# A four-layer trunk on one core: where residual, raw weights and split weights of the up products lie in SBUF, and five weight buffers in place of six

## The chip, the core and the metric

The kernel runs on one core of a Trainium2 chip. A core has TensorE (PE: matmuls from SBUF into PSUM; PEld is its loading of the stationary operand), VectorE (DVE), ScalarE (ACT), GpSimd (POOL) and SyncE (SP). SP, POOL and ACT also issue DMA transfers. Each engine works through its own instructions in order and waits for the others through semaphores. The metric is the device time of one execution in microseconds.

## What is computed

```python
# x: (1, 512, 1024) float32; two layers, mixer 0 = MLA, mixer 1 = GLA
for i in range(2):
    xn = rms_norm(x, norm_mix[i])
    x = x + (mla_mixer(xn, ...) if i % 2 == 0 else gla_mixer(xn, ...))
    x = x + sq_relu_mlp(rms_norm(x, norm_mlp[i]), mlp_w_up[i], mlp_w_down[i])
return rms_norm(x, final_norm)

def sq_relu_mlp(xn, w_up, w_down):          # w_up (1024, 4096), w_down (4096, 1024)
    return jnp.square(jax.nn.relu(xn @ w_up)) @ w_down
```

All is float32. The change lies in the two MLPs and in where some tiles lie.

## The kernel before, in words

**Numbers as two parts.** TensorE is fed tiles of a rounded type (F32R). A float32 tile is split in two: ACT copies it into the rounded type (`hi`, L104), DVE subtracts that from the source (`lo`, L107). A product of two such pairs is three matmuls: hi by hi, hi by lo, lo by hi (L112 to L114, and the same in L939, L948 and elsewhere). Weights come by DMA as float32 into `wraw` (`load`, L132, two buffers of 8 KB a partition) or, in the MLPs, into `comb` buffers; `piece` (L137) splits them into a pair of tiles `wh`, `wl`, of which there are three pairs of 4 KB tiles, taken in turns. A split for one product therefore waits until the product three before it is done.

**The pools.** Tiles are laid out from the low end of SBUF: `const` (among it the residual `xall`, 16 KB a partition, L155), then `sb` (wraw, wh, wl, `set_A` for activations' two parts, `set_B`, `tmp`, `acc` and small ones), and behind it whatever stage is running: the pools of MLA, `fast0` of the first MLP, the pool of GLA, `fast1` of the second MLP.

**An MLP.** 512 hidden columns make a block, of which there are eight. The first block's up product is done plainly (`up_first`, L846). Then come seven steps (`step`, L951). A step makes the up product of block b+1 and the down product of block b, each of them a 2 by 2 product of quadrants worked out with seven products in place of eight (a Strassen-Winograd scheme); sums of quadrants are formed on DVE, or by a transfer that adds to what is there (POOL, `accum_op=ALU.add`, L918 and L928). A step has 14 products, in turns up and down:

1 up a11, 2 down d11, 3 up a12, 4 down d12, 5 up a11 (now S1 + a11) with T2, 6 down d11 (now dS1 + d11), 7 up S1 with T1, 8 down d12 (now d11 + d12), 9 up a12 (now a11 + a12), 10 down dS3, 11 up s3 with T3, 12 down dS1, 13 up a22 with T4, 14 down d22.

An up product (`up_product`, L931) is 24 matmuls, L939, with 256 columns of a moving activation and a stationary weight tile. The moving tile is a `set` tile in 1, 3 and 9 and a `T` tile in 5, 7, 11 and 13. A down product (`down_product`, L941) is 12 matmuls, L948, with 512 columns of a moving weight tile and a stationary activation.

T1 to T4 are sums of the normed input's quadrants. `quadrants` (L864) forms them once in each MLP: float32 values t1 to t4 first (L873 to L877), in the buffers comb 2 to 5, then `signed` splits each (L828, L829) into the tiles T2, T3, T1, T4.

**The weights of a step.** Six comb buffers hold six of the pieces (S1, dS1, d11, d12, dS3, d22); A1 and A2 (1 MB each) go through wraw. `home` says which piece is in which buffer (L911). S1, dS1, dS3 and A2 have a second transfer that is added to the first, on POOL's queue. When a piece's last reader in a step has been issued, `after(name)` (L1098) fetches a piece of the next step into its buffer, by the table `NEXT` (L1056); the plain transfers go through SP's queue in the order of these calls. Before the first step the pieces are fetched in the order of the list in L1051; the first MLP also writes the residual to DRAM there (L1054), since the residual's own tile then serves for the sums S11, S12, SU, S21 (L814). A fifth sum, S5, has a tile of its own (L815).

**Ends of an MLP.** In the last step `before_next` (first MLP, L1070) or `at_the_end` (second, L1080) fetches other things into buffers that come free: the residual kept in DRAM, or the last block's down weights and the final gain. The last block is then done plainly: L1126 to L1136 in the first MLP, where L1135 adds the kept residual; `row` (L1162) in the second.

**GLA.** `pairs` (L1392) copies with a mask; the mask is an integer copy of the identity, `ident_i` (L1669). L1515 and, in `states`, L112 to L114 are matmuls with 256 columns there, on tiles S, qd, ADh, ADl, kth, ktl of its pool.

The order of the instructions on each engine, and the buffers that tiles get, come from a planner that walks the program with a model of the times; where it finds a product's operands late it puts another one first.

Of the kernel before, what the change touches and what calls it, by code (L numbers as in the profile page):

```python
# [50 lines left out]
def trunk_kernel(ctx: ExitStack, tc: tile.TileContext, t_in: dict, out: bass.AP):  # L51
# [4 lines left out]
    sb = ctx.enter_context(tc.tile_pool(name="sb", bufs=1))  # L56
    count = [0]
# [97 lines left out]
    xall = const.tile([P, ND, S], F32, name="xT")  # L155
# [218 lines left out]
    def mla(layer, nrm, first, pools):  # L374
# [37 lines left out]
        raw = sb.tile([P, ND, 256], F32, tag="wraw", bufs=2, name=uname("wraw"))  # L412
# [54 lines left out]
        raw = sb.tile([P, 2, MH, VD], F32, tag="wraw", bufs=2, name="wraw_v")  # L467
# [61 lines left out]
        raw = sb.tile([P, 3, MH, ROPE], F32, tag="wraw", bufs=2, name="wraw_qr")  # L529
# [18 lines left out]
        def project(h, tag="a"):  # L548
            if h % 4 == 0:
                raw = sb.tile([P, 3, 4, NOPE], F32, tag="wraw", bufs=2, name=uname("wraw_qn"))  # L550
# [3 lines left out]
                raw = sb.tile([P, 2, 4, NOPE], F32, tag="wraw", bufs=2, name=uname("wraw_kn"))  # L554
# [244 lines left out]
    def mlp(layer, nrm, nxt=None):  # L799
# [64 lines left out]
        def quadrants():  # L864
# [4 lines left out]
            t1, t2, t3, t4 = (by_k(comb(i), KH) for i in range(2, 6))  # L869
# [8 lines left out]
            for name, t, sign in (("T2", t2, -1.0), ("T3", t3, 1.0), ("T1", t1, -1.0), ("T4", t4, -1.0)):  # L878
                parts = fast.tile([P, KH, 2, TH], F32R, tag=name, name=uname(name))
                signed(t, parts[:, :, 0], parts[:, :, 1], sign)  # L880
                quad[name] = [parts[:, k] for k in lead]
# [29 lines left out]
        home = {"S1": 0, "dS1": 1, "d11": 4, "d12": 3, "dS3": 2, "d22": 5}  # L911
# [19 lines left out]
        def up_product(t, a, q, start):  # L931
            w = piece(a, KH, 256)
# [7 lines left out]

        def down_product(t, a, parts, start):  # L941
            wh, wl = piece(a, 2, 512)
# [8 lines left out]
        def step(b, q, r, after):  # L951
# [23 lines left out]
            d11, d12, ds1, ds3, d22 = (W[n] for n in ("d11", "d12", "dS1", "dS3", "d22"))  # L975
# [68 lines left out]
            onto("d", S21, d22, parts_of_quad(q21, -1.0), opening)  # L1044
# [25 lines left out]
        def before_next(name):  # L1070
            if name in ("d11", "S1", "d12", "dS3"):
                t = by_k(comb(home[name]), 2)
                SP.dma_start(t, x_kept[:, 2 * len(kept) : 2 * len(kept) + 2])
                kept.append(t)
            if name in ("A1", "A2"):
                last_raw.append(load(down_cols(len(last_raw)), 4, 512))
            if name == "dS1":
                DVE.tensor_tensor(S12, S12, S5, ALU.add)

        def at_the_end(name):  # L1080
            if name in ("d11", "S1", "d12", "dS3"):
                i = len(last_raw)
                t = by_k(comb(home[name]), 2)
                k0 = (NB - 1) * FB + i % 2 * 256
                SP.dma_start(t, w_dn[k0 : k0 + 256, i // 2 * 512 : (i // 2 + 1) * 512].rearrange("(k p) n -> p k n", p=P))
                last_raw.append(t)
            if name == "dS1":
                DVE.tensor_tensor(S12, S12, S5, ALU.add)
                t = comb(home[name])
                SP.dma_start(t, t_in["fin_row"].to_broadcast([P, D]))  # L1090
                gain.append(t)
                rounded(0)
# [16 lines left out]
        if nxt:  # L1109
# [5 lines left out]
            DVE.scalar_tensor_tensor(SU, SU, -1.0, S5, ALU.mult, ALU.subtract)  # L1115
# [27 lines left out]
        DVE.tensor_tensor(SU, SU, S5, ALU.add)  # L1143
# [53 lines left out]
    def gla(layer, nrm, vtag, ytag):  # L1197
# [165 lines left out]
        def levels(h):  # L1363
# [28 lines left out]
            def pairs():  # L1392
# [4 lines left out]
                def evacuate(p, a):  # L1397
                    DVE.copy_predicated(a, ident_i.unsqueeze(1).to_broadcast([P, 2, P]), p[:, :, :P])
# [232 lines left out]
    raw0 = sb.tile([P, ND, 256], F32, tag="wraw", bufs=2, name="wraw_ckv")  # L1631
# [37 lines left out]
    ident_i = const.tile([P, P], I32, name="ident_i")  # L1669
    DVE.tensor_copy(ident_i, ident)  # L1670
# [73 lines left out]
```

## Time and profile before

| | |
|---|---|
| median of 3 runs | 1057.02 us (1056.98 to 1057.12) |
| the profiled execution | 1057.37 us, of which its span 1055.6 us |
| TensorE clock granted | 0.999 |
| MLA and its output projection, up to the first MLP's steps | 0 to 206 us |
| steps of the first MLP | 206 to 480 us, 39 us each |
| GLA and its output projection | 505 to 752 us |
| steps of the second MLP | 753 to 1027 us |
| last block and final norm | 1027 to 1055.6 us |

How rows are read: a row of instructions has line, engine, operation, out<-in by the tiles' names, shapes and count, then busy time in us, mean ns of one, and idle time of the engine just before with what ended it. A row of a timeline begins with start and duration in us and ends with the idle time before it in brackets. "PE ps L939 x24" in the chain of waits is a run of 24 matmuls with the time from the first start to the next piece. A row of a window has its length, then PE, PEld, DVE, ACT and POOL busy time, then clock, share of DMA engines and GB/s.

### The profile page before, as it was taken

The page shows a single profiled execution, that of the slowest core. Times are in us where ns is not written, and L with a number is a line of the kernel's source. Part 1 is how long each engine was busy: PE and PEld are TensorE (multiplying, and loading weights), DVE is VectorE, ACT ScalarE, POOL GpSimd, SP SyncE. Part 2 cuts the span into 40 slices and gives each one's busy share as a digit, 9 for nine tenths or more (in the row PEclk, how much of TensorE's full clock was granted, in tenths as well). Part 3 has the DMA queues.
Part 4 walks back from the last instruction along what each step waited for, and adds up shares of the span by engine and source line. Part 5 has one row for each costly group of instructions (what it writes and reads, how often), then busy time and mean ns, then how long its engine had stood idle before and what let it go on. Part 6 is the DMA issues. An engine that isn't in the chain of part 4 may idle for free.

```text
span 1055.6 us, 15598 instructions
## 1 busy us (share of the span) xinstructions
PE 1045.5 (99%) x5966; PEld 913.7 (87%) x5966; DVE 876.0 (83%) x1340; ACT 698.6 (66%) x1074; POOL 113.4 (11%) x128
## 2 busy tenths in 40 slices
PE   9999999999999999999999999999999999999997
PEld 7888888889999999998888888878889999999985
DVE  7899977979889889898686498469889989989993
ACT  7667664577777767766445565655667777777784
POOL 7410011201101111000000000000011010010000
PEclk9999999999999999999999999999999999999999
DMA  7311235866966976842322221444496696696622
GB/s 231 90 51 41 81 79 160 238 176 150 235 181 150 229 192 146 221 147 93 90 80 80 80 80 51 126 105 132 110 248 132 178 254 140 176 249 152 165 81 80
DMA packets 120493, 149.97 MB, mean 142 GB/s; under 512 B 9345, under 2 KB 86145, under 8 KB 120289
## 3 DMA queue, kind: packets, MB, share of 16 engines
q1 hardware_dynamic: 95920, 117.76, 34.4%
q0 software_dynamic: 22400, 29.36, 17.4%
q10 hardware_dynamic: 2096, 1.84, 0.6%
q8 instruction: 47, 0.77, 0.3%
q14 instruction: 30, 0.24, 0.1%
HBM read 144.49 MB, written 4.19 MB: 141 GB/s over the span
## 4 chain that ended last, share of the span: by engine, by line
PE 95%; ACT 2%; DVE 2%; issue 0%; DMA 0%; ACTq 0%; SPq 0%; DVEq 0%
PE ps L939 26%; PE ps L948 25%; PE ps L112 10%; PE ps L114 10%; PE ps L113 10%; PE ps L1133 2%; PE ps L1388 2%; PE ps L129 1%; PE ps L1168 1%; PE ps L408 1%; PE ps L1515 1%; DVE wl L107 0%; PE ps L671 0%; PE ps L1438 0%; PE ps L667 0%
## 5 line engine op out<-in xcount | busy, mean ns | idle before, releaser
L948 PE MATMUL ps<-wh,set 128*128 128x512 f32 x784 | 258.5, 390 | 0.0
L107 DVE TENSOR_TENSOR wl<-wraw,wh 128x1024 fp32r<-128x1024 f32 x139 | 169.4, 1221 | 39.7 <-ACT wh L104 39.4
L104 ACT ACTIVATE wh<-wraw 128x1024 fp32r<-128x1024 f32 x139 | 145.9, 1053 | 82.1 <-PE ps L113 38.3
L948 PEld LDWEIGHTS ps<-wh,set 128*128 128x128 f32 x784 | 147.3, 188 | 28.8
L104 ACT ACTIVATE wh<-comb 128x1024 fp32r<-128x1024 f32 x112 | 118.8, 1061 | 62.8 <-PE ps L939 41.9
L939 PE MATMUL ps<-T,wh 128*128 128x256 f32 x896 | 159.8, 279 | 0.0
L948 PE MATMUL ps<-wl,set 128*128 128x512 f32 x392 | 153.7, 392 | 0.0
L107 DVE TENSOR_TENSOR wl<-comb,wh 128x1024 fp32r<-128x1024 f32 x112 | 136.7, 1220 | 18.6 <-ACT wh L104 16.9
L939 PEld LDWEIGHTS ps<-T,wh 128*128 128x128 f32 x896 | 140.5, 188 | 4.5
L939 PE MATMUL ps<-T,wl 128*128 128x256 f32 x448 | 125.1, 279 | 1.0 <-DVE wl L107 1.0
L939 PE MATMUL ps<-set,wh 128*128 128x256 f32 x672 | 122.6, 283 | 0.0
L939 PEld LDWEIGHTS ps<-set,wh 128*128 128x128 f32 x672 | 107.4, 191 | 3.2
L112 PE MATMUL ps<-set,wh 128*128 128x512 f32 x280 | 109.3, 392 | 0.7 <-ACT set L1557 0.3
L113 PE MATMUL ps<-set,wh 128*128 128x512 f32 x280 | 109.4, 391 | 0.0
L114 PE MATMUL ps<-set,wl 128*128 128x512 f32 x280 | 109.0, 390 | 0.0
L939 PE MATMUL ps<-set,wl 128*128 128x256 f32 x336 | 95.2, 283 | 0.0
L939 PEld LDWEIGHTS ps<-T,wl 128*128 128x128 f32 x448 | 84.2, 188 | 1.5 <-DVE wl L107 1.4
L948 PEld LDWEIGHTS ps<-wl,set 128*128 128x128 f32 x392 | 73.8, 188 | 11.6
L928 POOL DMA_DIRECT2D comb<-in_mlp_w_down_dram x28 | 33.6, 1201 | 421.0 <-DMA comb<-in_mlp_w_down_dram 155.5
L939 PEld LDWEIGHTS ps<-set,wl 128*128 128x128 f32 x336 | 64.3, 191 | 0.0
L112 PEld LDWEIGHTS ps<-set,wh 128*128 128x128 f32 x280 | 52.5, 188 | 12.6 <-ACT wh L104 1.0
L114 PEld LDWEIGHTS ps<-set,wl 128*128 128x128 f32 x280 | 52.6, 188 | 11.2 <-DVE wl L107 0.4
(396 smaller groups left out, 2024.2 us busy)
## 6 DMA issues: line engine op xcount, KB each, us to landing
comb<-in_mlp_w_down_dram SPq DMA_DIRECT2D x74, 512.0 KB, 5.0
wraw<-in_mlp_w_up_dram SPq DMA_DIRECT2D x32, 1024.0 KB, 5.8
comb<-in_mlp_w_down_dram POOLq DMA_DIRECT2D x28, 512.0 KB, 7.7
wraw<-in_gla_w_in_dram SPq DMA_DIRECT2D x12, 1024.0 KB, 5.3
comb<-in_mlp_w_up_dram SPq DMA_DIRECT2D x14, 512.0 KB, 3.8
comb<-in_mlp_w_up_dram POOLq DMA_DIRECT2D x14, 512.0 KB, 8.4
wraw<-in_mlp_w_up_dram POOLq DMA_DIRECT2D x14, 512.0 KB, 7.2
wraw<-in_mla_w_o_dram SPq DMA_DIRECT2D x4, 1024.0 KB, 5.0
```

The source lines that it names most:

```text
L104: order(ACT.activation(hi, src, AF.Copy))
L107: lo_eng.tensor_tensor(lo, src, f(hi), ALU.subtract)
L112: PE.matmul(psum, wh, xh, start=start, stop=False)
L113: PE.matmul(psum, wh, xl, start=False, stop=False)
L114: PE.matmul(psum, wl, xh, start=False, stop=stop)
L129: PE.transpose(psum, src, ident[: src.shape[0], : src.shape[0]])
L408: PE.matmul(p, w[:, i, j * P : (j + 1) * P], x, start=start, stop=stop)
L928: POOL.dma_start(t, q(b, *more), accum_op=ALU.add)
L939: PE.matmul(o, a_, x_, start=start and j == 0 and k == 0 and n == 0, stop=k == KH - 1 and n == 2, skip_group_check=True)
L948: PE.matmul(o, x_, w_, start=start and k == 0 and n == 0, stop=k == 1 and n == 2, skip_group_check=True)
L1133: PE.matmul(p, a, x, start=False, stop=k == 3 and n == 2, skip_group_check=True)
L1388: PE.matmul(p[:, t - t0], k[:, t * P : (t + 1) * P], moving[:, t], start=True, stop=True)
```

## The change

A new pool `far` at SBUF's high end holds the residual and both wraw buffers; a pool `up0` or `up1` below it, for the time of an MLP, holds two pairs `uh`, `ul` for the split weights of up products. In them lie t1 to t4 first. The down products' weights go in turns into two pairs of wh, wl that `hold` takes once in each MLP; the third pair holds the sum S5 and the buffer comb 4. There are five comb buffers; d22 is fetched into d11's buffer in the same step, and the table `NEXT` is another. At the ends, what is fetched where changes with it: in the second MLP the last block's second half of down weights goes through wraw. In GLA the mask is the identity's own bits, and `ident_i` is gone.

```diff
+    far = ctx.enter_context(tc.tile_pool(name="far", bufs=1, side="right"))
...
-        raw = sb.tile([P, a, n], F32, tag="wraw", bufs=2, name=uname("wraw"))
+        raw = far.tile([P, a, n], F32, tag="wraw", bufs=2, name=uname("wraw"))
...
-    xall = const.tile([P, ND, S], F32, name="xT")
+    xall = far.tile([P, ND, S], F32, name="xT")
...
+        ups = es.enter_context(tc.tile_pool(name=f"up{layer}", bufs=1, side="right", reuse_waits="tile"))
...
-        sums.append(fast.tile([P, 2 * S], F32, tag="sum", name="sum5"))
-        S11, S12, SU, S21, S5 = sums
+        S11, S12, SU, S21 = sums
+        held = {}
 
         def comb(i):
+            if i == 4:
+                return held["comb"]
             return fast.tile([P, 2 * S], F32, tag=f"comb{i}", bufs=1, name=uname("comb"))
+
+        def hold():
+            pairs = [[sb.tile([P, 2 * S], F32R, tag=tag, bufs=3, name=uname(tag)) for tag in ("wh", "wl")] for _ in range(3)]
+            held["down"] = pairs[:2]
+            held["S5"], held["comb"] = (f(t) for t in pairs[2])
+
+        def up_room(tag):
+            return ups.tile([P, 2 * S], F32R, tag=tag, bufs=2, name=uname(tag))
...
-            t1, t2, t3, t4 = (by_k(comb(i), KH) for i in range(2, 6))
+            room = {name: fast.tile([P, KH, 2, TH], F32R, tag=name, name=uname(name)) for name in ("T2", "T3", "T1", "T4")}
+            t3, t2, t1, t4 = (by_k(f(up_room(tag)), KH) for tag in ("uh", "ul", "uh", "ul"))
...
-        home = {"S1": 0, "dS1": 1, "d11": 4, "d12": 3, "dS3": 2, "d22": 5}
+        home = {"S1": 0, "dS1": 1, "d11": 2, "d12": 3, "dS3": 4}
...
         def up_product(t, a, q, start):
-            w = piece(a, KH, 256)
+            w = tuple(by_k(up_room(tag), KH) for tag in ("uh", "ul"))
+            split(a, *w)
...
+        downs = []
+
         def down_product(t, a, parts, start):
-            wh, wl = piece(a, 2, 512)
+            room = held["down"][len(downs) % 2]
+            downs.append(a)
+            wh, wl = (by_k(t_, 2) for t_ in room)
+            split(a, wh, wl)
...
         up_first(Q[0])
+        hold()
         quadrants()
...
-        for name in ("S1", "dS1", "d11", "A1", "d12", "dS3", "A2", "d22"):
+        for name in ("S1", "dS1", "d11", "A1", "d12", "dS3", "A2"):
...
-        NEXT = {"d11": "dS1", "S1": "S1", "d12": "d11", "A1": "A1", "dS3": "d12", "dS1": "dS3", "A2": "A2", "d22": "d22"}
+        NEXT = {"d11": "d22", "S1": "d11", "d12": "S1", "A1": "A1", "dS3": "dS1", "dS1": "d12", "A2": "A2", "d22": "dS3"}
...
-        def before_next(name):
-            if name in ("d11", "S1", "d12", "dS3"):
-                t = by_k(comb(home[name]), 2)
+        def before_next(name, at):
+            if name in ("S1", "d12", "dS3", "dS1"):
+                t = by_k(comb(at), 2)
                 SP.dma_start(t, x_kept[:, 2 * len(kept) : 2 * len(kept) + 2])
...
         for b in range(NB - 1):
             final = b == NB - 2
-            old = dict(home)
+            old = dict(home, d22=home["d11"])
 
             def after(name, b=b, final=final, old=old):
-                if final:
-                    return before_next(name) if nxt else at_the_end(name)
                 new = NEXT[name]
-                if name in home:
+                if new == "d22":
                     home[new] = old[name]
-                fetch(b + 1, new)
+                    fetch(b, new)
+                elif final:
+                    (before_next if nxt else at_the_end)(name, old.get(name))
+                else:
+                    if name in old:
+                        home[new] = old[name]
+                    fetch(b + 1, new)
...
-                    DVE.copy_predicated(a, ident_i.unsqueeze(1).to_broadcast([P, 2, P]), p[:, :, :P])
+                    DVE.copy_predicated(a, ident.bitcast(I32).unsqueeze(1).to_broadcast([P, 2, P]), p[:, :, :P])
...
-    ident_i = const.tile([P, P], I32, name="ident_i")
-    DVE.tensor_copy(ident_i, ident)
```

More of the change, by code (lines that the diff above doesn't have):

```diff
@@ L411, in mla @@
         KH = ND // 2
-        raw = sb.tile([P, ND, 256], F32, tag="wraw", bufs=2, name=uname("wraw"))
+        raw = far.tile([P, ND, 256], F32, tag="wraw", bufs=2, name=uname("wraw"))
         wq = []
@@ L464, in mla @@
         rsqrt(rows, means, S, row_eps)
-        raw = sb.tile([P, 2, MH, VD], F32, tag="wraw", bufs=2, name="wraw_v")
+        raw = far.tile([P, 2, MH, VD], F32, tag="wraw", bufs=2, name="wraw_v")
         for k in range(2):
@@ L526, in mla @@
         DVE.tensor_tensor(kt, ka, pk3[:, :, ROPE:], ALU.add)
-        raw = sb.tile([P, 3, MH, ROPE], F32, tag="wraw", bufs=2, name="wraw_qr")
+        raw = far.tile([P, 3, MH, ROPE], F32, tag="wraw", bufs=2, name="wraw_qr")
         for k in range(3):
@@ L549, in project @@
             if h % 4 == 0:
-                raw = sb.tile([P, 3, 4, NOPE], F32, tag="wraw", bufs=2, name=uname("wraw_qn"))
+                raw = far.tile([P, 3, 4, NOPE], F32, tag="wraw", bufs=2, name=uname("wraw_qn"))
                 for k in range(3):
@@ L553, in project @@
                 wn["raw"] = raw
-                raw = sb.tile([P, 2, 4, NOPE], F32, tag="wraw", bufs=2, name=uname("wraw_kn"))
+                raw = far.tile([P, 2, 4, NOPE], F32, tag="wraw", bufs=2, name=uname("wraw_kn"))
                 for k in range(2):
@@ L878, in quadrants @@
             for name, t, sign in (("T2", t2, -1.0), ("T3", t3, 1.0), ("T1", t1, -1.0), ("T4", t4, -1.0)):
[L879 removed]
+                parts = room[name]
                 signed(t, parts[:, :, 0], parts[:, :, 1], sign)
@@ L974, in step @@
             a11, a12, s3, a22 = A1[:, :KH], A1[:, KH:], A2[:, :KH], A2[:, KH:]
-            d11, d12, ds1, ds3, d22 = (W[n] for n in ("d11", "d12", "dS1", "dS3", "d22"))
+            d11, d12, ds1, ds3 = (W[n] for n in ("d11", "d12", "dS1", "dS3"))
+            S5 = held["S5"]
             z = bank("u")
@@ L1042, in step @@
             after("A2")
-            onto("d", S21, d22, parts_of_quad(q21, -1.0), opening)
+            onto("d", S21, W["d22"], parts_of_quad(q21, -1.0), opening)
             after("d22")
         up_first(Q[0])
+        hold()
         quadrants()
@@ L1114, in mlp @@
             DVE.scalar_tensor_tensor(S21, S21, -1.0, SU, ALU.mult, ALU.subtract)
-            DVE.scalar_tensor_tensor(SU, SU, -1.0, S5, ALU.mult, ALU.subtract)
+            DVE.scalar_tensor_tensor(SU, SU, -1.0, held["S5"], ALU.mult, ALU.subtract)
             for c in range(2):
@@ L1142, in mlp @@
         DVE.tensor_tensor(S21, S21, SU, ALU.add)
-        DVE.tensor_tensor(SU, SU, S5, ALU.add)
+        DVE.tensor_tensor(SU, SU, held["S5"], ALU.add)
         rounded(1)
@@ L1629, in gla @@
         return Y, begun[0]
-    raw0 = sb.tile([P, ND, 256], F32, tag="wraw", bufs=2, name="wraw_ckv")
+    raw0 = far.tile([P, ND, 256], F32, tag="wraw", bufs=2, name="wraw_ckv")
     src0 = t_in["mla_w_in"][0][:, QL : QL + KL].rearrange("(k p) n -> p k n", p=P)
```

21 lines of the change are left out of this document (12 added, 9 removed).

## The prediction, made before the changed kernel ran

> **What bounds the kernel now.** I read the page first, then the chain of waits, then what TensorE itself waited for.
>
> ```profile
> span 1055.6 us, 15598 instructions
> PE 1045.5 (99%) x5966; PEld 913.7 (87%) x5966; DVE 876.0 (83%) x1340; ACT 698.6 (66%) x1074; POOL 113.4 (11%) x128
> PE 95%; ACT 2%; DVE 2%; issue 0%; DMA 0%; ACTq 0%; SPq 0%; DVEq 0%
> ...
> PE ps L1652 <- DVE ones L168: 1.2, 1, 1.2
> PE ps L939 <- DVE wl L107: 1.0, 2, 0.5
> PE ps L408 <- ACT set L249: 0.4, 1, 0.4
> PE ps L112 <- ACT set L1557: 0.3, 1, 0.3
> ```
>
> TensorE is busy all the time, 95% of the chain is TensorE, and what it waited for itself adds up to some 3 us, 1.2 of them at the very start. So the change can win in two ways only: by taking away one of these few waits, or by letting the matmuls follow one another faster. It can lose much more, by letting DVE, ACT or a transfer come late, since DVE too is busy 83% of the span.
>
> Of the waits, one lies where the diff is: L939, the up product, twice, once in each MLP. Here are the two places in TensorE's order of time.
>
> ```profile
> 214.10 0.40 PE L939 MATMUL ps<-T,wh 128*128 128x256 f32 x2
> 215.01 0.39 PE L939 MATMUL ps<-T,wl 128*128 128x256 f32 x1 [0.51 <-DVE wl L107]
> 215.24 0.39 PE L939 MATMUL ps<-T,wh 128*128 128x256 f32 x2
> ...
> 761.27 0.40 PE L939 MATMUL ps<-T,wh 128*128 128x256 f32 x2
> 762.20 0.39 PE L939 MATMUL ps<-T,wl 128*128 128x256 f32 x1 [0.53 <-DVE wl L107]
> 762.42 0.40 PE L939 MATMUL ps<-T,wh 128*128 128x256 f32 x2
> ```
>
> Starts, not durations, tell the pace of a pipelined TensorE. A whole product of 24 such matmuls takes 2.80 us (the chain's row at 223.37 below), so 0.117 us each. From 214.10 to 215.01 there are 2 matmuls: 0.91 where 0.23 is due, and the next one takes 0.23 for 0.12. The loss is 0.68 + 0.11 = 0.79 us; at 761.27 it is 0.70 + 0.10 = 0.80. Together **1.6 us**.
>
> **The change part by part.**
>
> *Split weights of the up products in two pairs of buffers of their own (uh, ul), those of the down products in two held pairs.* Before, all products took turns in three pairs (wh, wl), so the split for a product waited for the product three before it. What this does to the wait at 214 is seen in the work ahead of it.
>
> ```profile
> 205.77 2.87 PE ps L939 x24
> 208.65 2.54 PE ps L948 x11
> ...
> 211.20 0.63 ACT L104 ACTIVATE set<-set 128x512 fp32r<-128x512 f32 x1 [1.09 <-PE ps L948]
> 211.74 1.01 ACT L985 ACTIVATE xT<-ps 128x1024 f32<-128x1024 f32 x1
> 212.65 1.05 ACT L104 ACTIVATE wh<-wraw 128x1024 fp32r<-128x1024 f32 x1
> 213.73 1.23 DVE L107 TENSOR_TENSOR wl<-wraw,wh 128x1024 fp32r<-128x1024 f32 x1 [0.49 <-ACT wh L104]
> ```
>
> The first step's products are: up 205.77 to 208.64, down 208.65 to 211.2, up 211.2 to 214.1, then the T2 product that stalls. Its weights go into the pair of the down product, free at 211.2; ACT comes to them at 212.65, DVE ends at 214.96, TensorE needed them at 214.1 + 0.23. In the changed kernel they go into the pair of the first up product, free at 208.64: earliest end 208.64 + 1.05 + 1.23 = 210.9, over 3 us early. The down weights of this step find their pairs free as soon as the up_first products that had them are done, so ACT and DVE can also split them earlier. The stall should go: -1.6 us. Bounds: 0 (ACT keeps its order, L985 ahead of the split) to -1.6. I take **-1.5**.
>
> Against it stands that the up pairs are filled first with t1 to t4, the temporaries of quadrants(), which lay in comb 2 to 5. The first up split now waits until T2 and T3 are made, the second until T1 and T4 are. In the trace of before the last of these ends at 189.91 + 3.48 = 193.4, and the first split by DVE for the step begins later (196.82 is up_first's last and then the step's first):
>
> ```profile
> 189.91 3.48 DVE L829 SCALAR_TENSOR_TENSOR T<-comb,T 128x1024 fp32r<-128x1024 f32 x3
> 196.82 2.35 DVE L107 TENSOR_TENSOR wl<-wraw,wh 128x1024 fp32r<-128x1024 f32 x2
> ```
>
> So this costs 0, with over 3.4 us of cover; if the cover went, the price would be at most a split's 1.05 + 1.23.
>
> *Where the tiles lie.* The rows of the same matmul with different tiles differ, with no wait between:
>
> ```profile
> 223.37 2.80 PE ps L939 x24
> 228.91 2.87 PE ps L939 x24
> ...
> L939 PE MATMUL ps<-T,wh 128*128 128x256 f32 x896 | 159.8, 279 | 0.0
> L939 PE MATMUL ps<-set,wh 128*128 128x256 f32 x672 | 122.6, 283 | 0.0
> L939 PE MATMUL ps<-T,wl 128*128 128x256 f32 x448 | 125.1, 279 | 1.0 <-DVE wl L107 1.0
> L939 PE MATMUL ps<-set,wl 128*128 128x256 f32 x336 | 95.2, 283 | 0.0
> L1515 PE MATMUL ps<-S,qd 128*128 128x256 f32 x36 | 4.9, 279 | 0.0
> L1515 PE MATMUL ps<-set,ADh 128*128 128x256 f32 x32 | 5.8, 280 | 0.0
> L1515 PE MATMUL ps<-set,ADl 128*128 128x256 f32 x16 | 4.5, 282 | 0.0
> L112 PE MATMUL ps<-set,kth 128*128 128x256 f32 x12 | 3.4, 280 | 0.0
> ```
>
> A product whose moving operand is a set tile takes 2.87 us, one with a T tile 2.80: 0.07 us in 24 matmuls, 3 ns each. By the sizes in the code, set, wh and wl all start 32 bytes off a multiple of 64; the T tiles and everything in the pools behind start on one (S, qd, AD, kth). So "both operands off" has 283, and every pairing with one or both on a multiple of 64 has 279 to 282. The change puts the stationary uh and ul on multiples of 64 (far end, sizes of 4096, 8192 and 16384 bytes), and leaves set off and T on. The nearest rows for set with uh are set with ADh, ADl and kth: 280, 282, 280, weighted 280.5, which is 2.5 ns under 283; 672 + 336 = 1008 matmuls make -2.5 us. The nearest for T with uh is S with qd: 279 as now, but that row is short and rounded; 1 ns on 896 + 448 = 1344 matmuls would be +1.3. That the address is the cause is my reading of these rows; it could as well be the tile's shape, and then the term is 0. Bounds: -3.0 (set at T's pace) to +5.4 (T at set's pace, 4 ns on 1344). I take -2.5 and a third of the 1.3: **-2.0**. The down products, wh and set as before, keep their pace.
>
> The Trainium skill's page SBUF — State Buffer (section Who interferes with whom) says that PE and ACT never wait on anyone, and places contention in one shared port pair of two other engines. By that rule no placement changes a matmul's pace and this term is 0; the rows 279 and 283 don't bear it out to the last per cent.
>
> *Five weight buffers in place of six.* d22 of a step is fetched when d11's buffer is free in the same step, and every other piece moves one place on. In a steady step the releases and needs are these.
>
> ```profile
> 284.70:323.70 39.00, 39.00 (x254) 35.56 (x254) 34.85 (x39) 28.34 (x36) 4.97 (x4) 1.00 0.74 188
> ...
> 296.00 0.37 SPq L926 DMA_DIRECT2D comb<-in_mlp_w_down_dram  x1
> 306.58 6.29 SPq L926 DMA_DIRECT2D comb<-in_mlp_w_down_dram  x2
> ...
> 315.40 1.06 ACT L104 ACTIVATE wh<-comb 128x1024 fp32r<-128x1024 f32 x1 [0.45 <-PE ps L939]
> 325.79 1.22 DVE L994 TENSOR_TENSOR comb<-comb,comb 128x1024 f32<-128x1024 f32 x1
> ...
> comb<-in_mlp_w_down_dram SPq DMA_DIRECT2D x74, 512.0 KB, 5.0
> DMA to landing us min/median/max: 5.7/8.1/11.4
> ```
>
> d22: issued at 296.0 (there dS1 was), landed 5.0 later at 301.0, split at 315.4: 14 us to spare. dS1 moves from 296.0 to dS3's release, 306.58, and is the tightest: plain part until 311.6, accumulated part (POOL's, the landing row) at worst 11.4 more, 323.0; L994 adds it at 325.79. That leaves 2.8 us, and 6 by the median. S1, d12 and dS3 move by 2 to 6 us and keep over 8. On SP's queue d22 stands first in its step, and nothing that waits is put ahead of it. In an MLP's first step dS3's buffer is a held one, free when up_first's last product ends at 205.6, so SP holds A2 behind it until then; A2 is used some 10 products of 2.8 us later. Cost 0; if a piece came late, DVE would stand still with every split behind it.
>
> *S5 and the fifth buffer in the third pair.* At the end of MLP 0 the kept residual for the last two tiles lies in that pair, so one wl fewer is free when the next stage's first weights are split.
>
> ```profile
> 500.75 1.23 DVE L107 TENSOR_TENSOR wl<-wraw,wh 128x1024 fp32r<-128x1024 f32 x1 [0.21 <-ACT wh L104]
> 505.90 0.68 DVE L1135 TENSOR_TENSOR xT<-ps,comb 128x512 f32<-128x512 f32 x1
> ```
>
> The split at 500.75 may then wait for L1135's last add and end at about 505.90 + 0.68 + 1.23 = 507.8, where TensorE turns to these products at about 505.1. It has the pair's other half to do meanwhile (7 tiles of 3 matmuls, 4.8 us). Bounds 0 to 507.8 - 505.8 = 2; I take **+0.3**.
>
> *The rest:* the copy into ident_i goes, a DVE instruction shorter than the 0.68 above, where DVE isn't on the chain: 0. Residual and unsplit weights move without change of size; ACT and DVE, which read them, aren't the bound: 0.
>
> Sum: -1.5 - 2.0 + 0.3 = -3.2 on the profiled execution's 1057.37 us: 1054.2. The median shown, 1057.02, is 0.35 under it, so the forecast is **1053.8 us**.
>
> **The rivals.**
>
> A, the pace stays: set's 283 is due to something else than the address, as the skill's rule has it; only the stalls go. For it: only 108 matmuls in the rows show the other pairing. 1057.02 - 1.5 + 0.3 = 1055.8.
>
> B, the pace gains, the stalls stay, because ACT's fixed order still has the split behind L985, or another one takes its place: 1057.02 - 2.0 + 0.3 = 1055.3.
>
> C, slower by pace: T lies lower and uh in the far end, and the T products fall to 2.87. 4 of 7 up products in each of 14 steps are T's: 56 x 0.07 = +3.9, on top of A: 1059.7. Against it: S with qd, both on multiples of 64, has 279. It decides from 1 ns a matmul on.
>
> D, slower by starvation: dS1's accumulated part, now issued 10 us later and right behind S1's on POOL's queue, lands after L994 wants it. From 311.6 it has 14.2 us, and TensorE has one product's lead of about 2.8, so from 17 us on each further us costs 1 us in each of 12 steps; 18 us would make +12, 1068. Against it: the maximum 11.4.
>
> **How the numbers follow.** Forecast 0.43, A 0.25, B 0.15, C 0.10, D 0.07. The range reaches from all gains at their bounds (1057.02 - 1.6 - 3.0 = 1052.4, and a little) to C: 1052.2 to 1059.8; D is left out. The forecast's own range is 1052.2 to 1055.0. This kernel's runs agree within 0.02%, but the line between a change and none is put at 0.2%, 2.1 us: 1054.9 and 1059.1. Faster: the forecast but for its upper edge, and the lower edge of B, 0.45; same 0.38; slower, C and D, 0.17.
>
> **What would show it.** The wait L939 on DVE wl gone from TensorE's list and 24 matmuls of the first T2 product in 2.80: the first step right. The chain's pieces of L939 all at 2.80 (283 become 280): the second; some still at 2.87: A; all at 2.87: C. A wait of DVE L994 on a DMA of comb, and TensorE waiting for wl once in each step: D. The forecast is wrong if TensorE waits anywhere for over a us that it doesn't wait now.

## The result, and the profile after

The changed kernel takes 1060.32 us (median of 7 runs, 1059.48 to 1062.82) against 1057.02 us before: ratio 1.0036, 95% interval 1.0026 to 1.0046. It is **slower by about 3 us**, where 1053.8 us was forecast and 1059.8 us was the upper end of the range. Run once more later, beside other kernels, it took 1059.22 us (10 runs, 1058.63 to 1060.71), ratio 1.0022 (1.0013 to 1.0031). The profiled execution took 1060.31 us, so it stands for the first median.

From the page of the changed kernel (the lines that answer to those shown of before; L953 is the up product that was L939, L967 the down product that was L948):

```profile
span 1058.6 us, 15619 instructions
...
PE 1048.3 (99%) x5966; PEld 915.9 (87%) x5966; DVE 873.8 (83%) x1339; ACT 702.4 (66%) x1074; POOL 113.1 (11%) x128
...
PE 92%; DVE 3%; ACT 2%; DMA 1%; issue 1%; ACTq 0%; SPq 0%; DVEq 0%
...
L953 PE MATMUL ps<-T,uh 128*128 128x256 f32 x896 | 163.4, 281 | 0.0
...
L953 PE MATMUL ps<-T,ul 128*128 128x256 f32 x448 | 126.3, 282 | 0.0
...
L953 PE MATMUL ps<-set,uh 128*128 128x256 f32 x672 | 120.6, 279 | 0.0
...
L953 PE MATMUL ps<-set,ul 128*128 128x256 f32 x336 | 94.0, 280 | 0.0
```

DVE does less and TensorE as many matmuls as before, and still TensorE is busy 2.8 us longer. The two kinds of up products have changed places: 279 and 283 ns for T and set before, 281 to 282 and 279 to 280 ns now.

What TensorE itself waited for, in the changed kernel:

```profile
PE ps L1680 <- DVE ones L169: 1.2, 1, 1.2
PE ps L115 <- DVE wl L108: 0.9, 1, 0.9
PE ps L967 <- ACT ps L976: 0.5, 1, 0.5
PE ps L113 <- ACT set L1585: 0.3, 1, 0.3
```

The wait of the up product on DVE's wl, 1.0 us before, has left the list. Two others have come: L115 (a projection of GLA) on wl, and L967 (a down product) on ACT.

The chain of waits of the changed kernel in the first MLP's first steps (start, length, what):

```profile
205.87 2.82 PE ps L953 x24
208.70 2.73 PE ps L967 x12
...
222.84 2.87 PE ps L953 x24
225.71 2.76 PE ps L967 x12
228.47 2.82 PE ps L953 x24
231.29 2.73 PE ps L967 x12
```

Compare the pieces of before: 223.37 was a T product of 2.80 and 228.91 a set product of 2.87, and the down products behind them were these.

```profile
226.17 2.75 PE ps L948 x12
231.78 2.75 PE ps L948 x12
```

Now the same two up products take 2.87 and 2.82, and the down products 2.76 and 2.73. From 205.77 to 223.37 were 17.60 us, from 205.87 to 222.84 are 16.97. So the MLP's start is 0.63 us shorter; in it the two set products are 0.05 us faster each and the T2 product is 0.07 us slower.

The starts of the matmuls in the traces cut the span into stretches. Differences to the profiled execution of before, in us ("first" is the first three pairs of products, both MLPs together; "later" is all behind it in an MLP's steps; "GLA" from the end of MLP 1's steps to the first up product of MLP 2):

| kernel | to the 1st product | first | later, MLP 1 | later, MLP 2 | GLA | end | sum |
|---|---|---|---|---|---|---|---|
| changed | +0.10 | -1.26 | +1.26 | +1.63 | +1.09 | +0.22 | +3.0 |
| changed, again | +0.83 | -1.24 | +0.89 | +1.33 | +1.21 | +0.07 | +3.1 |
| residual in d22's buffer | +0.32 | -1.24 | +2.07 | +0.89 | -0.07 | +0.08 | +2.0 |
| dS1 asked for earlier | -0.33 | -1.27 | +0.89 | +0.89 | -0.05 | +0.07 | +0.2 |

In the two columns "later" 0.89 stands four times, and nothing lower: that is the matmuls' pace, 1.78 us for both MLPs. What is above it (0.36 and 0.74 in the changed kernel, 0.44 in its repetition, 1.17 with the residual moved) comes and goes by execution: single stalls. So the 3.0 us are **pace +1.8, single stalls +1.1, the start of GLA +1.1, the MLPs' starts -1.3**, and 0.3 at both ends.

### The profile page after: what moved, and what is told of

Same layout as the page of the kernel before. It is cut to its first block, busy times and chain, and to the rows that moved or that the text cites. A ratio compares the mean times of both kernels' runs of the same rounds, so it can differ in the third digit from the quotient of the medians.

```text
span 1058.6 us, 15619 instructions
## 1 busy us (share of the span) xinstructions
PE 1048.3 (99%) x5966; PEld 915.9 (87%) x5966; DVE 873.8 (83%) x1339; ACT 702.4 (66%) x1074; POOL 113.1 (11%) x128
## 4 chain that ended last, share of the span: by engine, by line
PE 92%; DVE 3%; ACT 2%; DMA 1%; issue 1%; ACTq 0%; SPq 0%; DVEq 0%
PE ps L953 25%; PE ps L967 24%; PE ps L115 10%; PE ps L113 10%; PE ps L114 10%; PE ps L1416 2%; PE ps L130 1%; PE ps L1196 1%; PE ps L1161 1%; PE ps L409 1%; DMA comb<-in_mlp_w_down_dram 1%; PE ps L1543 1%; DVE wl L108 1%; PE ps L1466 0%; PE ps L672 0%
## 5 line engine op out<-in xcount | busy, mean ns | idle before, releaser
L967 PE MATMUL ps<-wh,set 128*128 128x512 f32 x784 | 258.9, 391 | 0.5 <-ACT ps L976 0.5
L967 PEld LDWEIGHTS ps<-wh,set 128*128 128x128 f32 x784 | 147.0, 188 | 30.2 <-ACT ps L976 0.9
L953 PE MATMUL ps<-T,uh 128*128 128x256 f32 x896 | 163.4, 281 | 0.0
L967 PE MATMUL ps<-wl,set 128*128 128x512 f32 x392 | 153.6, 392 | 0.0
L953 PEld LDWEIGHTS ps<-T,uh 128*128 128x128 f32 x896 | 142.2, 189 | 4.2
L953 PE MATMUL ps<-T,ul 128*128 128x256 f32 x448 | 126.3, 282 | 0.0
L105 ACT ACTIVATE uh<-wraw 128x1024 fp32r<-128x1024 f32 x84 | 89.1, 1061 | 48.5 <-PE ps L953 42.4
L953 PE MATMUL ps<-set,uh 128*128 128x256 f32 x672 | 120.6, 279 | 0.0
L108 DVE TENSOR_TENSOR ul<-wraw,uh 128x1024 fp32r<-128x1024 f32 x84 | 102.5, 1220 | 21.2 <-ACT uh L105 20.9
L115 PE MATMUL ps<-set,wl 128*128 128x512 f32 x280 | 109.1, 391 | 0.9 <-DVE wl L108 0.9
L953 PEld LDWEIGHTS ps<-set,uh 128*128 128x128 f32 x672 | 105.5, 188 | 3.1
L953 PE MATMUL ps<-set,ul 128*128 128x256 f32 x336 | 94.0, 280 | 0.0
L953 PEld LDWEIGHTS ps<-T,ul 128*128 128x128 f32 x448 | 83.8, 187 | 0.1
L967 PEld LDWEIGHTS ps<-wl,set 128*128 128x128 f32 x392 | 73.6, 188 | 11.9
L108 DVE TENSOR_TENSOR wl<-wraw,wh 128x1024 fp32r<-128x1024 f32 x55 | 66.9, 1219 | 18.1 <-ACT wh L105 18.0
L113 PEld LDWEIGHTS ps<-set,wh 128*128 128x128 f32 x280 | 52.5, 188 | 12.6 <-ACT wh L105 1.0
```

The lines of the kernel that those rows point to most:

```text
L105: order(ACT.activation(hi, src, AF.Copy))
L108: lo_eng.tensor_tensor(lo, src, f(hi), ALU.subtract)
L113: PE.matmul(psum, wh, xh, start=start, stop=False)
L115: PE.matmul(psum, wl, xh, start=False, stop=stop)
L953: PE.matmul(o, a_, x_, start=start and j == 0 and k == 0 and n == 0, stop=k == KH - 1 and n == 2, skip_group_check=True)
L967: PE.matmul(o, x_, w_, start=start and k == 0 and n == 0, stop=k == 1 and n == 2, skip_group_check=True)
```

## The experiments

All are edits of the changed kernel unless said otherwise. The kernel before ran beside all of them, at 1057.0 to 1057.3 us.

### Shifting the weights of the up products by 32, 64, 96 and 128 bytes

The compiled kernels tell where the tiles lie. Modulo 128 bytes: before, wh and wl at 32, set at 32, T at 64. In the changed kernel set and T are where they were modulo 128, and uh and ul lie at 96: the tiles at the far end are laid down from byte 229344 of a partition, and that is 32 off a multiple of 64. There are three theories: the pace depends on the difference between weight's and moving operand's start (phase), on the weights being at the far end (place), or on the weights' own alignment.

```diff
             room = {name: fast.tile([P, KH, 2, TH], F32R, tag=name, name=uname(name)) for name in ("T2", "T3", "T1", "T4")}
             t3, t2, t1, t4 = (by_k(f(up_room(tag)), KH) for tag in ("uh", "ul", "uh", "ul"))
+            DVE.memset(ups.tile([P, 8], F32, tag="pad", name=uname("pad")), 0.0)
```

with 8, 16, 24 and 32 floats. On every engine the order of the instructions stays that of the changed kernel, but for this memset. In what follows a product's time is taken from the start of its first matmul to the start of its last, which is 23 intervals of 24; hence the factor 24/23 where whole products are priced.

> 32 bytes are put behind the up products' weight buffers, so that these start 32 bytes lower; nothing else moves. Phase theory: the time from the first to the last of the 24 matmuls of an up product depends on the difference, modulo 128 bytes, between the start of the weights and that of the moving operand. In the two kernels traced so far it was 2686 ns at -32, 2752 ns at 0, 2751 ns at +32 and 2709 ns at 64. Here the products over T come to 0 (2752 ns, as in the changed kernel) and those over the set to +32 (2709 to 2751 ns): 42 x 0.042 x 24/23 = 1.8 us slower than the changed kernel. Place theory (what counts is that the weights lie at the far end, not their low address bits): 2751 and 2709 ns stay, no change of time. Own-alignment theory (a moving operand's or a weight's own start counts, not the difference): the set's and T's products would change by the same amount, or not at all.

> 64 bytes in place of 32. Phase theory: T's products come to -32 and fall from 2751 to 2686 ns (56 x 0.065 x 24/23 = -3.8 us), the set's come to 0 and rise from 2709 to 2752 ns (+1.9 us): the pace of the kernel before, 1.9 us faster than the changed kernel. Place theory: no change of pace or time. Own-alignment theory: both kinds change in the same direction.

> 96 bytes. Phase theory: T's products come to -64, which is 64, and take 2709 ns in place of 2751 (-2.4 us), the set's come to -32 and take 2686 in place of 2709 (-1.0 us): 3.4 us faster than the changed kernel, about the time of the kernel before. Place theory: no change. Own-alignment theory (weights' own start at a multiple of 128 is what counts): both kinds take the same time.

> 128 bytes behind the up products' weights: the differences modulo 128 are again those of the changed kernel (T 32, set 64), modulo 256 they are 32 and 64 in place of 160 and 192. Phase theory with a period of 128: 2751 and 2709 ns, to some 15 ns, and the time of the changed kernel (1059.2 us beside the last runs) within 1 us: the pad by itself costs and brings nothing. With a period of 256: T's products at 32 were never measured; the set's at 64 take 2639 ns, as T's did, 42 x 0.070 x 24/23 = 3.1 us less.

Measured, with all the other placements that ran (start of a product's first matmul to start of its last, the median of 56 T and 42 set products; nearly all agree within 1 ns; "difference" is the weight's start less the moving operand's, modulo 256):

| kernel | T: difference, ns | set: difference, ns | later steps, us, without single stalls, per MLP | median, us |
|---|---|---|---|---|
| before | 224, 2686 | 0, 2752 | 0 | 1057.0 |
| changed | 160, 2751 | 192, 2709 | +0.89 | 1060.32, 1059.22 |
| 32 bytes | 128, 2733 | 160, 2757 | +1.38 | 1060.71 |
| 64 bytes | 96, 2705 | 128, 2764 | +2.07 | 1062.02 |
| 96 bytes | 64, 2639 | 96, 2702 | -0.81 | 1056.45 |
| 128 bytes | 32, 2715 | 64, 2709 | +0.01 | 1057.94 |
| moving operands shifted | 96, 2697 | 224, 2685 | -0.74 | 1056.50 |
| before, T shifted 96 bytes | 128, 2753 | 0, 2752 | +2.52 | 1062.22 |

The place theory is out: nothing but bytes of padding moves the time between 1056.45 and 1062.02 us. The weights' own alignment is out too: with 32 bytes the weights start on a multiple of 64, and with the same weights the set products are slower for it (2709 to 2757) and T's faster (2751 to 2733). The phase theory holds in the large: differences of 0 and 32 modulo 128 give 2715 to 2764 ns, 64 and 96 give 2639 to 2709, in all sixteen. In the small it doesn't: the period of 128 is exact for the set products at 64 and 192 (2709 both), but T's at 32 and 160 differ by 36 ns, and equal differences with other layouts differ by up to 31 at 128 (2733, 2764, 2753) and by 70 at 64 (T with 96 bytes 2639, set with 128 bytes 2709). So the difference tells slow placements from fast ones, but not how fast a placement is.

The expectations for 32 and 128 bytes were met in part. With 32 bytes 1.8 us were expected on top of the changed kernel, and the steps took 2 x (1.38 - 0.89) = 1.0 us longer: the set's products rose by 48 ns, a little more than the bound of 42, but T's fell by 18 where nothing was expected. With 128 bytes the set's 2709 came as the period of 128 has it, and not the 2639 of a period of 256; but T's fell by 36 ns where some 15 were allowed, and the pace is 1.8 us better than the changed kernel's where it should have been the same.

For **64 bytes the expectation was wrong, in sign**: 1.9 us faster, 0.95 in each MLP, and the kernel is 1.17 us an MLP slower than the changed one. The chain of waits of that kernel shows why (T, down, set, down):

```profile
222.48 2.82 PE ps L954 x24
225.30 2.78 PE ps L968 x12
228.08 2.89 PE ps L954 x24
230.97 2.77 PE ps L968 x12
```

T's products are faster than in the changed kernel (by 46 ns, not 65) and the set's slower (by 55, not 43): 0.8 us of the miss of 2.1 in an MLP. The rest is in the *down* products: they take 2.78 and 2.77 behind T and set where they took 2.76 and 2.73, with their own tiles where they were. An MLP has 49 of them, 28 behind T's: 28 x 0.02 + 21 x 0.04 = 1.4 us. With 96 bytes they pay as much:

```profile
222.75 2.76 PE ps L954 x24
225.51 2.78 PE ps L968 x12
228.29 2.81 PE ps L954 x24
231.11 2.77 PE ps L968 x12
```

There the sum was met to the tenth, 1.70 us in each MLP, and by luck, since its parts were not as expected: T's products gain 112 ns where 42 stood, and the down products give half of it back. Within a down product the matmuls start 224 to 240 ns apart at first and 226 to 231 at the end, in every kernel; what the up product ahead leaves behind wears off on the way. So an up product's phase is paid twice, in itself and in its follower, and the expectations had only the first.

### Shifting the moving operands, in the changed kernel and in the kernel before

```diff
-    eps_t = const.tile([P, 1], F32, name="eps_t")
+    eps_one = const.tile([P, 2], F32, name="eps_one")
+    eps_t, one_t = eps_one[:, :1], eps_one[:, 1:]
...
-    one_t = const.tile([P, 1], F32, name="one_t")
...
+            DVE.memset(fast.tile([P, 24], F32, tag="pad", name=uname("pad")), 0.0)
             room = {name: fast.tile([P, KH, 2, TH], F32R, tag=name, name=uname(name)) for name in ("T2", "T3", "T1", "T4")}
```

> Here the weights of the up products stay where the change put them (96 modulo 128), and the moving operands are shifted: T to 0 in place of 64, the set to 0 in place of 32, by a pad ahead of T and by one constant less. Phase theory (the difference of the two starts counts): both kinds come to -32 modulo 128 (96 and 224 modulo 256), where 2686 and 2705 ns were measured: T falls from 2751 to between 2686 and 2705, the set from 2709 to between 2686 and 2705, 2.7 to 4.8 us less in the up products; with the products behind them at +-1.9 us, as in the run with 64 bytes, 0.8 to 6.7 us faster than the changed kernel. Own-alignment theory (the weights' start decides, the moving operand's doesn't): 2751 and 2709 ns, no change.

1056.50 us (1055.74 to 1058.36), 2.7 us below the changed kernel that ran beside it. T's products take 2697 ns, the set's 2685; the down products behind them are back at 2.75. (With the constant gone everything in `sb` starts 32 bytes lower, the down products' weights and their set too, both at 0 in place of 32 modulo 128, so their 2.75 is no clean test of what stands ahead of them.)

```profile
222.36 2.81 PE ps L954 x24
225.18 2.75 PE ps L968 x12
227.93 2.80 PE ps L954 x24
230.73 2.75 PE ps L968 x12
```

The weights didn't move by a byte, so it is not their start alone: the moving operand's start acts as theirs does. The set at 224, with starts of 0 and 96 modulo 128, has T's value of before to 1 ns (2685 and 2686, there with starts of 64 and 32).

The second test puts the loss into the kernel before, by a pad of 96 bytes ahead of its T tiles:

```diff
             for name, t, sign in (("T2", t2, -1.0), ("T3", t3, 1.0), ("T1", t1, -1.0), ("T4", t4, -1.0)):
                 parts = fast.tile([P, KH, 2, TH], F32R, tag=name, name=uname(name))
```

(with the line `DVE.memset(fast.tile([P, 24], F32, tag="pad", name=uname("pad")), 0.0)` ahead of the loop)

> The kernel before, with 96 bytes put ahead of the four tiles T1 to T4 and nothing else. Its up weights lie at the near end in the shared buffers. Phase theory: T's products, at a difference of -32 in the kernel before (2686 ns), come to 128 of 256 bytes, where 2733 and 2764 ns were measured: 56 x (0.047 to 0.078) x 24/23 = 2.7 to 4.6 us slower than the kernel before, with the set's products at 2752 ns as they were; the loss of the change, without the change. Place theory (the far end makes T's products slow): 1057.1 us, T's products at 2686 ns.

1062.22 us (1061.78 to 1062.84), ratio 1.0050 (1.0036 to 1.0064): 5.2 us slower than before. The kernel before with T shifted, in the chain of waits (T, down, set) and in the groups:

```profile
222.96 2.88 PE ps L940 x24
225.84 2.76 PE ps L949 x12
228.60 2.87 PE ps L940 x24
```

```profile
L940 PE MATMUL ps<-T,wh 128*128 128x256 f32 x896 | 163.6, 282 | 0.0
L940 PE MATMUL ps<-T,wl 128*128 128x256 f32 x448 | 127.6, 285 | 1.0 <-DVE wl L107 1.0
L940 PE MATMUL ps<-set,wh 128*128 128x256 f32 x672 | 122.6, 283 | 0.0
```

T's 2.80 us have become 2.88, with no far end and three shared pairs of weight buffers. Of the 2.7 to 4.6 us expected, T's own share is 56 x 0.067 x 24/23 = 3.9; the rest is again in the down products, 2.76 behind T for 2.75 (19 ns each by the starts, 1.1 us for 56).

### The start of the GLA projections

In the changed kernel the fourth pair of residual tiles is read back into the held buffer, which is the wl of the third pair. The timeline there:

```profile
506.31 0.68 DVE L1163 TENSOR_TENSOR xT<-ps,wl 128x512 f32<-128x512 f32 x1
...
506.91 0.39 PE L113 MATMUL ps<-set,wh 128*128 128x512 f32 x1
506.92 1.21 DVE L108 TENSOR_TENSOR wl<-wraw,wh 128x1024 fp32r<-128x1024 f32 x1
...
508.18 0.50 PE L115 MATMUL ps<-set,wl 128*128 128x512 f32 x1 [0.89 <-DVE wl L108]
```

The split into that wl starts right behind the residual's last addition from it, and TensorE, out of other work at 507.3, waits for it: 0.89 us by the row, 1.05 by the starts (1.27 apart, where 0.23 is usual).

```diff
         def before_next(name, at):
-            if name in ("S1", "d12", "dS3", "dS1"):
+            if name in ("S1", "d12", "dS3", "d22"):
```

> The fourth residual pair that is read back in the last step of the first MLP goes into d22's buffer in place of the third pair's lower half. Theory: the stall of 1.05 us at the start of the GLA projections, where the first pieces wait for the third pair, goes; -1.0 us against the changed kernel, pace of the products as in it. Rival: the projections' start waits for something else that is as late (the last residual's addition itself, or the weights' load), and the time changes by less than 0.3 us.

1057.97 us (1057.22 to 1059.41): 1.25 us below the repetition of the changed kernel. What TensorE waited for in this kernel:

```profile
PE ps L1680 <- DVE ones L169: 1.2, 1, 1.2
PE ps L967 <- ACT ps L976: 0.9, 1, 0.9
PE ps L113 <- ACT set L1585: 0.3, 1, 0.3
```

L115's wait is gone, and the stretch "GLA" of the table falls from +1.09 to -0.07. Against the first runs of the changed kernel it was 2.35 us, more than its stall; that question went into a repetition.

> The changed kernel once more, beside the others on one chip. The run with the fourth residual in d22's buffer was 2.35 us faster than the changed kernel's first runs (1060.32 us), of which its profile explains 1.05 us. If the rest is the scatter of those first runs, the median here is 1059 us, 1.0 to 1.3 us above that run; if the place of the residual is worth all of it, 1060.3 us again.

1059.22 us. Its profile has the wait of L115 (0.9 us) as before. So the residual's buffer is worth the 1.1 us that its profile shows, and the remaining 1.1 us lie between two sets of runs of the same kernel.

### The order in which the five buffers are filled

A single stall of the changed kernel in its timeline. dS1's plain transfer is one of the two on SP's queue, its accumulated part POOL's; then DVE's addition, ACT and TensorE:

```profile
892.90 5.35 SPq L939 DMA_DIRECT2D comb<-in_mlp_w_down_dram  x2
...
900.44 1.19 POOL L941 DMA_DIRECT2D comb<-in_mlp_w_down_dram  x1 [7.99 <-DVE ul L108]
...
911.92 1.22 DVE L1014 TENSOR_TENSOR wl<-comb,wl 128x1024 f32<-128x1024 f32 x1 [1.94 <-DMA comb<-in_mlp_w_down_dram]
...
919.45 1.01 ACT L976 ACTIVATE ps<-ps 128x1024 f32<-128x1024 f32 x1
...
920.50 0.50 PE L967 MATMUL ps<-wh,set 128*128 128x512 f32 x1 [0.46 <-ACT ps L976]
```

From the plain part's issue to the addition are 19.0 us. DVE stands still for 1.94 us, is late with all that follows, and three products later TensorE waits: 0.46 us by the row, 0.6 by the starts of its matmuls (0.73 apart, where 0.12 is usual).

```diff
-        NEXT = {"d11": "d22", "S1": "d11", "d12": "S1", "A1": "A1", "dS3": "dS1", "dS1": "d12", "A2": "A2", "d22": "dS3"}
+        NEXT = {"d11": "d22", "S1": "dS1", "d12": "S1", "A1": "A1", "dS3": "d11", "dS1": "d12", "A2": "A2", "d22": "dS3"}
```

> Of the five buffers' order of fetching: dS1's weights are asked for behind S1 and d11's behind dS3, so that dS1's plain part and the part added to it leave some 8 us earlier; all else as in the changed kernel. Starvation theory: the waits of TensorE for dS1's split (0.7 us near 920 us and 0.3 us near 449 us in the changed kernel's profile, up to 1.4 us at another place in others) go, and with them the scatter of 3.3 us between runs: 0.5 to 1.5 us faster than the changed kernel's 1060.3 us, runs within 1 us of each other. Rival: the waits move to d11 or S1, which are now asked for later; time and scatter as in the changed kernel.

1057.73 us (1057.16 to 1058.71), 1.5 us below the repetition of the changed kernel. What TensorE waited for in this kernel:

```profile
PE ps L1680 <- DVE ones L169: 1.2, 1, 1.2
PE ps L409 <- ACT set L250: 0.6, 1, 0.6
PE ps L113 <- ACT set L1585: 0.3, 1, 0.3
```

No wait of L967, and DVE's L1014 waits for no transfer any more. But L115's wait has gone as well: with this order the held buffer belongs to dS3 in the last step, so it takes the third residual in place of the fourth and is free earlier. The stall at GLA's start is 1.1 of the 1.5 us. That leaves 0.2 to 0.4 us for the stalls in the median, less than the 0.5 to 1.5 expected from the profiles; 7 of the 9 profiles with the change's order have one (0.4 to 1.5 us), none of the three with this order. The runs lie 1.55 us apart, where 1 was expected.

### Together

The 96 bytes or the shifted operands, the fourth residual in d22's buffer, and with the other order of filling the residuals read back behind S1, d12, dS1 and d22.

> The weights of the up products start 96 bytes lower, and the fourth residual pair is read back into d22's buffer. If the two effects are independent, the median is that with the 96 bytes alone less the stall of 1.05 us at the start of the GLA projections: 1056.45 - 1.05 = 1055.4 us. If the run with the residual alone was 2.35 us faster for another reason (its profile still has a stall of 1.0 us at 449 us), 1054.1 us.

> Both of these and dS1's weights asked for earlier (the fourth residual's addition keeps its place). Starvation theory: 0.5 to 1.4 us below the run with both alone, 1054.0 to 1054.9 us, and runs within 1 us of each other. Rival (the waits only move): as the run with both alone, 1055.4 us.

> The shifted moving operands with the fourth residual in d22's buffer and dS1's weights asked for earlier. Independent effects: 1056.5 - 1.05 (start of the GLA projections) - 0 to 1.1 (starved stalls; the profile with the shift alone has one of 1.1 us) = 1054.4 to 1055.5 us, within 1 us of the run with 96 bytes and both (1054.43 us); runs within 1.7 us of each other.

| kernel | median, us | runs | ratio to before |
|---|---|---|---|
| 96 bytes, residual | 1054.57 | 11, 1054.09 to 1057.24 | 0.9983 (0.9974 to 0.9992) |
| 96 bytes, residual, order | 1054.43 | 9, 1054.01 to 1055.68 | 0.9977 (0.9968 to 0.9987) |
| operands, residual, order | 1054.51 | 8, 1053.93 to 1054.87 | 0.9973 (0.9963 to 0.9983) |

From the page of the last:

```profile
span 1053.1 us, 15629 instructions
```

With the five buffers of the change and all it fetches, it is 2.8 us faster than before and 4.7 us faster than the changed kernel's repetition. With the 96 bytes the parts did not add up to what was expected: the first kernel of the table is 0.8 us below the 1055.4 of independent effects and 0.5 above the 1054.1 of the other sum. Its profile has GLA's start 1.1 us shorter, as it should be, and what the rest of the median is due to isn't shown. The order brought 0.1 us in the median there, where 0.5 to 1.4 were expected, and its runs lie 1.7 us apart in place of 1. With the shifted operands the sum came within its bounds, with 0.9 us for the order (1056.50 - 1.05 - 1054.51). What the order does in both cases is to take away the slowest runs.

## Why the prediction was wrong, point by point

**The stalls at the MLPs' starts: right.** -1.5 was forecast; the first three pairs are 1.26 us shorter in sum, in which the two T2 products are 0.07 us slower and the four set products 0.05 us faster each. The up product's wait on wl is gone from TensorE's list.

**Where the tiles lie: the step that failed.** It gave -2.0 and the matmuls' pace came to +1.8. Of its two parts, set with uh was put at -2.5 and measured -1.9, which is near; T with uh was put at a third of 1.3 and measured +3.8. That part has the wrong size, and with it the sum has the wrong sign. The reasoning failed in three places. First, "the change puts the stationary uh and ul on multiples of 64": it puts them at 96 modulo 128, because the sizes were counted from an end taken to be a multiple of 64. Second, "both operands off has 283, and every pairing with one or both on a multiple of 64 has 279 to 282": what the rows showed was a difference of 0 (wh with set, 2752 ns) and of -32 (wh with T, 2686), and the rule about each operand's own start fitted those by chance; with 32 bytes of padding uh *is* on a multiple of 64, and set's products take 2757. Third, "the down products, wh and set as before, keep their pace": they took 2.73 and 2.76 for 2.75 here, little in sum, but up to 2.78 in the other placements. In the sum T's 56 products cost 56 x 0.065 x 24/23 = +3.8 us and the set's 42 bring 42 x 0.043 x 24/23 = -1.9 us. Rival C had the +3.9 for T, by another reason (T lying lower and uh in the far end, which the padding rules out), and had put 0.10 on it. That its 1059.7 us comes near the measured time is luck: it has neither the set's gain of 1.9 nor the stalls, which make up for it.

The rule quoted from the Trainium skill's SBUF — State Buffer (Who interferes with whom), that PE and ACT never wait on anyone, was read there as a term of 0. In these products TensorE waited on no other engine, so as a rule on engines it isn't touched; read as a rule on placement it doesn't hold, since TensorE's pace changes by up to 125 ns in 2.7 us with its own two operands' starts.

**Five buffers in place of six: cost 0 was forecast, 1.1 us were found in the profile, and some tenths in the median.** dS1 was rightly named the tightest, but the estimate took 5.0 us for its plain part, which is the median of its row, and 11.4 at worst behind it: 16.4 in sum, from 306.58 to 323.0. In the stall shown above it took 19.0 us from 892.90. The plain part landed after 7.0 us, at 899.88, the accumulated one was issued 7.5 us after it, and DVE could add 11.5 us later. So the accumulated part met the worst that was allowed, and the plain part took longer than the median. The need also came sooner: DVE was ready for the addition at 909.98, 17.1 us after the issue, where the estimate had 19.2 (325.79 - 306.58). Just ahead of each of the two parts 1 MB had been asked for on SP's queue (A1 at 888.80, A2 at 900.35); that this company made them slow is not shown. Rival D had this mechanism and its point (17 us), but took it to strike in each of 12 steps; in the changed kernel's profile DVE waits for dS1 four times, and it reaches TensorE in one or two steps.

**The held pair at GLA's start: the mechanism right, the size wrong.** +0.3 was taken out of bounds of 0 to 2; the row measures 0.89, the stretch +1.1. The prediction's own bound had the split's end at 507.8 (508.1 measured) and TensorE's work until 505.1 + 4.8; but the order put only six of the projection's matmuls ahead of the one that needs wl, until 507.3.

**The rest, at 0: right.** The end is 0.05 to 0.2 us longer; the stretch up to the first up product, which the change doesn't touch but for places, varies from -0.6 to +0.8 us over all profiles.

The forecast said that it would be wrong if TensorE waited anywhere for over a us that it doesn't wait now. It does, by 1.05 us at GLA's start, by the starts of its matmuls. Without that wait and the single stalls it would still have been some 4 us off, by the pace alone (+1.8 for -2.0).

## What to carry to other kernels

When a diff moves matmul operands, take their start addresses from the compiled program, not from sums of tile sizes, and compare the pace of whole products by matmul starts before and after; where TensorE is the bound, a pad of 32 to 128 bytes is worth a run of its own. When buffers are shared at a stage's end, follow the last reader of each to the first writer of the next stage. When one buffer fewer moves a transfer behind others, price both its parts at their slowest, and not one of them at its median.

## What the runs showed that was not expected

A matmul of 256 columns on rounded float32 takes 113 ns from start to start at best here, and 115 to 125 in most placements. The 24 of a product are 2639 to 2764 ns from the first start to the last. The start of the weight tile less that of the moving tile sorts them: 0 and 32 modulo 128 are slow, 64 and 96 fast. The pattern within a product repeats with a period of a few matmuls and carries into the next product. In the product with 2639 ns the intervals are 118, 120, 119, 123, 119 and then 113, with a 114 now and then, to the end, so it finds a state without loss; in the others it doesn't. That the reading of the next weights collides with the streaming of the moving tile would fit, and the Trainium skill's page TensorE: Matmul & The Clock Gate (section Step-by-step: what each phase is for) says the opposite, that loading the next tile's weights doesn't steal SBUF read bandwidth from the running matmul, since TensorE has a read port for each. The runs show only that moving either start changes the pace, not where the two streams meet. That stays open, as does what separates T from set tiles at equal differences (70 ns at 64), and why the down products pay more behind some placements than behind others.
